# Feed-forward pairs: 18 of 22 by seven half-width products on operands scaled by 1/rms, the first four plain

## The chip, the cores and the metric

The kernel runs on one core of one Trainium2 chip. The metric is the device time of one execution in microseconds (us); the time shown for the kernel before is the median of three runs. The profile is one further execution, taken by the hardware profiler. In it PE is TensorE (matmuls), PEld its weight loads, DVE is VectorE, ACT ScalarE, POOL GpSimd, SP the queue that issues DMAs.

## The reference

Two layers over 512 tokens of width 1024. Each layer adds half a feed-forward, then a mixer (sparse attention, spatial gating, two gated projections), then half a second feed-forward; a last RMSNorm follows. What the change touches is the feed-forward:

```python
def rmsnorm(x, g):
    y = x * rsqrt(mean(x * x, axis=-1, keepdims=True) + 1e-6)
    return y * g

def swiglu(h, w_gate_up, w_down):              # 1024 -> 2 * 2816 -> 1024
    g, u = split(h @ w_gate_up, 2, axis=-1)
    return (silu(g) * u) @ w_down

x = x + 0.5 * swiglu(rmsnorm(x, ffn1_norm[l]), ffn1_w_gate_up[l], ffn1_w_down[l])
```

## The kernel before

**Layout.** x stays in SBUF transposed: eight tiles (`x[:, k, :]`) of 128 features by 512 tokens. The 2816 hidden features are 22 blocks of 128; a *pair* is the gate block and the up block of one such index, and its 1024x256 weights come in one buffer `X` of 128x2048.

**Three products for one.** All large matmuls run on fp32r operands. Each operand is split in a high part (a rounding copy on ACT) and the rest (a subtraction on DVE; `split`), and a product is high x high, high x low and low x high, all summed in PSUM by `chain`. So each weight tile costs one ACT and one DVE instruction before TensorE can use it.

**Pairs.** `pair_plain` makes gate and up as two chains of 8 x 3 matmuls of 512 columns, 48 in all. DVE multiplies both by `rbc` (1/rms broadcast over the partitions), ACT takes Silu, GpSimd multiplies the two. `pair_seven` treats the pair as a product of 2x2 blocks by Strassen's scheme in Winograd's form: seven products of half the depth and half the tokens, each 4 x 3 matmuls of 256 columns, 84 in all. For it DVE also adds weight blocks (`Sm`, tile names W here: one add of 1024 and two of 512 columns) and splits them (three of 1024 and one of 512 columns, the last one into VL); four DVE additions join the products from PSUM in `TT` (names YB). GpSimd then multiplies `TT` by `rbc` in two instructions, ACT takes Silu, GpSimd multiplies gate by up. The input side of the seven products (`norm_sums`: four sums of halves for each of four tile pairs, split into `Th`, `Tl`) is made once a feed-forward, after pair 0, from two ACT copies scaled by the gain.

**Order.** The operand tiles `xh`, `xl` hold the input times the gain, without 1/rms, so that matmuls start before the norm is known. 22 pairs come in the groups of `CHUNKS`, (0,6), (6,12), (12,18), (18,22). After each group its rows of the down projection run: 8 output tiles, each a chain of 3 matmuls of 512 columns for every pair of the group, added to x by DVE. `SEVEN` says which pairs run by seven products: of every three the first two, from pair 4 on in the first layer-half and 3 in the others, up to 20. That is 11 or 12 of 22 and 47 of 88 in all; 41 are plain. In the last group every new x tile is squared (ACT) and added to `ss0` (GpSimd for tiles 1 to 5, DVE for 6 and 7; `norm_square`), and the next operands are made.

**The planner.** All instructions are recorded, and `order` issues them by a list schedule over all engines: among those that its cost model (`SBUF_COST`, `cost`) takes for ready, the earliest in program order, weight preparation 100 places early. Each engine then runs its list in that fixed order. Buffers are rings: weights use two `X`, one `Sm`, three high and three low tiles of 1024 columns and one pair of 512; PSUM has six banks for the pairs and two for the down projection.

Of the kernel before, what the change touches and what calls it, by code (L numbers as in the profile page):

```python
# [20 lines left out]
NT = 4  # L21
DEPTH = 2
NG = (3 * DEPTH + 1) * KD
CHUNKS = ((0, 6), (6, 12), (12, 18), (18, 22))
LAG = 1
AHEAD = 100
FIRST, LATER = 4, 3

def SEVEN(j, begins):

    return j % 3 < 2 and (FIRST if begins else LATER) <= j < 21


NEG = -1e30
# [5 lines left out]

SBUF_COST = {"DVE": (154, 1.05), "ACT": (205, 0.835), "POOL": (150, 3.2)}
TABLES = {AF.Silu: 1, AF.Gelu_apprx_tanh: 2, AF.Exp: 3, AF.Tanh: 3, AF.Sqrt: 4}


# [96 lines left out]
class Recorder:  # L145
# [31 lines left out]
    def note(self, engine, op, args, kw):  # L177
        outs = [v for v in [args[0], kw.get("accum_out")] if isinstance(v, View)]
        ins = [v for v in list(args[1:]) + [v for k, v in kw.items() if k != "accum_out"] if isinstance(v, View)]
        i, deps = len(self.ops), set()  # L180
        for v, writes in [(v, False) for v in ins] + [(v, True) for v in outs]:
            assert v.live(), v.buf.name
            q, e = v.region()
            keep = []
            for j, jw, jq, je in v.buf.log:
                if (writes or jw) and jq & q and je & e:
                    if j != i:
                        deps.add(j)
                    if writes and jq & ~q == 0 and je & ~e == 0:
                        continue  # L190
                keep.append((j, jw, jq, je))
            keep.append((i, writes, q, e))
            v.buf.log = keep
        self.ops.append((engine, op, args, kw, deps, i + self.bias.get(engine, 0) - self.ahead, self.cost(engine, op, args, kw, outs, ins)))

    def cost(self, engine, op, args, kw, outs, ins):

# [25 lines left out]
    def order(self):  # L223
        ops = self.ops
        users, left = [[] for _ in ops], [len(o[4]) for o in ops]
        for i, o in enumerate(ops):
            for j in o[4]:
                users[j].append(i)
        ready = [0.0] * len(ops)
        free = dict.fromkeys(self.real, 0.0)  # L230
        cand = {e: [] for e in self.real}
        table, out, dma = 0, [], 0.0
        for i, o in enumerate(ops):
            if not left[i]:
                cand[o[0]].append(i)
        while len(out) < len(ops):
            best = None
            for e, c in cand.items():
                if not c:
                    continue  # L240
                t = max(free[e], min(ready[i] for i in c))
                if best is None or t < best[0]:
                    best = t, e
            t, e = best
            i = min((i for i in cand[e] if ready[i] <= t), key=lambda i: ops[i][5])
            cand[e].remove(i)
            busy, lat = ops[i][6]
            if e == "ACT":
                f = next((a for a in list(ops[i][2]) + list(ops[i][3].values()) if a in TABLES), None) \
                    if ops[i][1] == "activation" else None  # L250
                if f is not None and TABLES[f] != table:
                    table, busy, lat = TABLES[f], busy + 1283, lat + 1283
            if e == "SP":
                dma = max(dma, t + 2000) + lat
                lat = dma - t
            free[e] = t + busy
            out.append(i)
            for u in users[i]:
                same = ops[u][0] == e
                ready[u] = max(ready[u], t + (busy if same and e != "SP" else lat + 70))  # L260
                left[u] -= 1
                if not left[u]:
                    cand[ops[u][0]].append(u)
        self.span = max(free.values())
        return out
# [14 lines left out]
def trunk(ctx: ExitStack, tc, d):  # L280
# [20 lines left out]
    def units(*bufs):  # L301
        return [(b, c) for b in bufs for c in range(0, b.cols, 1024)]

    def halves(*bufs):
        return [(b, c) for b in bufs for c in range(0, b.cols, 512)]

    for tag, places, cols, dtype in (
            ("Xraw", [(W[0], 0), (W[1], 0)], 2048, F32), ("Fraw", units(W[0], W[1]), 1024, F32),
            ("S", [(W[2], 0)], 2048, F32), ("T32", [(W[3], 0)], 1024, F32), ("Txa", [(W[4], 0)], S, F32), ("Txb", [(W[4], 512)], S, F32), ("ss0", [(W[4], 1536)], S, F32),
            ("Fhi", units(*WH), 1024, F32R), ("Flo", units(*WL), 1024, F32R),  # L310
            ("F22h", halves(V[1])[:2], S, F32R), ("F22l", halves(V[1])[2:], S, F32R),
            ("raw", units(W[0], W[1])[:3], 1024, F32), ("whi", units(*WH), 1024, F32R), ("wlo", units(*WL)[:2], 1024, F32R),
            ("raw5", units(W[0], W[1])[:3] + units(W[3]), 1024, F32), ("wlo3", units(*WL), 1024, F32R),
            ("whi5", units(*WH, RB[0], RB[1]), 1024, F32R), ("wlo5", units(*WL, RB[2], RB[3]), 1024, F32R),
            ("U", [(W[2], 0)], 2048, F32), ("pA", halves(W[3]), S, F32), ("pB", halves(W[4]), S, F32),
            ("ga", halves(W[1])[2:] + [(G, 0)], S, F32), ("diagh", [(WL[2], 0)], S, F32R), ("diagl", [(WL[2], 512)], S, F32R)):
        rec.over(tag, places, cols, dtype)
    for k in range(24):
        rec.over(f"R{k}", [(RB[k // 2], k % 2 * 512)], S, F32R)
    for k, place in enumerate([(b, 0) for b in RB[6:]] + units(V[0])):  # L320
        rec.over(("Th", "Tl")[k // 4] + str(k % 4), [place], 1024, F32R)
    rec.over("TT", units(YB), 1024)
    rec.over("tm", [p for p, *_ in [rec.rings["t"]]][0] + halves(W[4]), S)
    for k in range(KD):
        rec.ring(f"xh{k}", 1, S, F32R)
# [17 lines left out]
    def tt(name):  # L343
        return rec.tile(st["t"], [P, S])
# [49 lines left out]
    def norm_begin(gidx):  # L394
        st["g"] = gains[:, gidx * KD:(gidx + 1) * KD]
        st["xh"], st["xl"] = [None] * KD, [None] * KD
        st["Th"], st["Tl"] = [None] * 4, [None] * 4
        st["s"] = None

    def norm_square(k):  # L400

        if st["s"] is None:
            st["s"] = rec.tile("ss0", [P, S])
            act(st["s"], x[:, k, :], AF.Square)
        else:
            sq = tt("sq")
            act(sq, x[:, k, :], AF.Square)
            eng = pool if k < 6 else vec
            eng.tensor_tensor(st["s"], st["s"], sq, op=ALU.add)

    def norm_operand(k):
# [5 lines left out]
        act(xh, x[:, k, :], AF.Copy, scale=g)  # L417
        vec.scalar_tensor_tensor(xl, x[:, k, :], g, f(xh), op0=ALU.mult, op1=ALU.subtract)

    def norm_sums(q):  # L420

        t, xa, xb = rec.tile("T32", [P, 1024]), rec.tile("Txa", [P, S]), rec.tile("Txb", [P, S])
        act(xa, x[:, q, :], AF.Copy, scale=st["g"][:, q:q + 1])
        act(xb, x[:, q + 4, :], AF.Copy, scale=st["g"][:, q + 4:q + 5])
        n1, n2, t3, t4 = (t[:, n * 256:(n + 1) * 256] for n in range(4))
        vec.tensor_tensor(n1, xa[:, 0:256], xa[:, 256:512], op=ALU.subtract)
        vec.scalar_tensor_tensor(n2, xb[:, 256:512], -1.0, n1, op0=ALU.mult, op1=ALU.subtract)
# [83 lines left out]
        nb[0] += 1  # L511
        return bank(nb[0] % 6, "ps_gu")

    def pair_plain(w):
        out = []
        for p, q in (("21", "22"), ("11", "12")):
            ps = next_bank()
# [5 lines left out]
            chain(ps, ops)  # L523
            out.append(ps)
        g, u = tt("g"), tt("u")
        vec.tensor_tensor(g, out[0], rbc, op=ALU.mult)
        act(g, g, AF.Silu)
        vec.tensor_tensor(u, out[1], rbc, op=ALU.mult)
        pool.tensor_tensor(u, u, g, op=ALU.mult)
        return u  # L530

    def pair_seven(w):
# [33 lines left out]
        vec.tensor_tensor(L[:, 256:512], D[:, 0:256], R[:, 256:512], op=ALU.add)  # L566
        times(A[:, 256:512], "s1", "n1")
        vec.tensor_tensor(half(R), half(R), two(A[:, 256:512]), op=ALU.add)
        for v, r in ((L, rbc[:, 0:256]), (R, rbc[:, 256:512])):
            pool.tensor_tensor(half(v), half(v), two(r), op=ALU.mult)  # L570
        u = tt("u")
        t4 = TT.rearrange("p (a b c) -> p a b c", a=2, b=2)
        act(t4[:, :, 1, :], t4[:, :, 1, :], AF.Silu, scale=-1.0)
        pool.tensor_tensor(half(u), t4[:, :, 0, :], t4[:, :, 1, :], op=ALU.mult)
        return u

    def ffn(gu, dn, l, gnext):
        st["rings"] = ("Fraw", "Fhi", "Flo")
        norm_finish(7)
        for c0, c1 in CHUNKS:  # L580
            hh, hl = [], []
            for j in range(c0, c1):
                seven = SEVEN(j, gnext == 1)
                w = first.pop() if first else pair_split(pair_load(gu[l, j]), seven)
                u = (pair_seven if seven else pair_plain)(w)
                if j == 0:
                    for q in range(4):
                        norm_sums(q)
                h = rt(2 * (j % 6), "hh")
                lo = rt(2 * (j % 6) + 1, "hl")  # L590
                split(h, lo, u)
                hh.append(h)
                hl.append(lo)
            last = c1 == 22
            final = last and gnext == 3 * DEPTH
            nk, fin = c1 - c0, []
# [2 lines left out]
            for dd in range(KD):  # L599
# [21 lines left out]
                        norm_rows(fin[-1], lo // P, 2, sq)  # L621
                if last and not final:
                    norm_prep(dd)
            for half, ps in enumerate(fin):
                store(half, ps)

# [598 lines left out]
```

## Time and profile before

| | |
|---|---|
| three runs, median (range) | 2168.75 us (2167.99 to 2169.68) |
| profiled execution: time, span | 2171.32 us, 2169.4 us |
| granted TensorE clock, mean | 0.996 |
| PE, PEld, DVE, ACT, POOL busy | 99%, 85%, 70%, 47%, 17% |

The span reaches from the first to the last instruction; the execution's time is 1.9 us longer. Matmuls are pipelined and the end of each is modelled, so two matmuls in a row overlap in the trace: what one costs in a stream is the time from its start to the start of the next. The same holds in a smaller measure for DVE. All instructions carry line 276, since the planner issues them there; tiles tell them apart.

### The profile page before, as it was taken

The page shows a single profiled execution, that of the slowest core. Times are in us where ns is not written, and L with a number is a line of the kernel's source. Part 1 is how long each engine was busy: PE and PEld are TensorE (multiplying, and loading weights), DVE is VectorE, ACT ScalarE, POOL GpSimd, SP SyncE. Part 2 cuts the span into 40 slices and gives each one's busy share as a digit, 9 for nine tenths or more (in the row PEclk, how much of TensorE's full clock was granted, in tenths as well). Part 3 has the DMA queues.
Part 4 walks back from the last instruction along what each step waited for, and adds up shares of the span by engine and source line. Part 5 has one row for each costly group of instructions (what it writes and reads, how often), then busy time and mean ns, then how long its engine had stood idle before and what let it go on. Part 6 is the DMA issues. An engine that isn't in the chain of part 4 may idle for free.

```text
span 2169.4 us, 30061 instructions
## 1 busy us (share of the span) xinstructions
PE 2139.0 (99%) x11704; PEld 1849.9 (85%) x11704; DVE 1518.8 (70%) x2357; ACT 1011.9 (47%) x1635; POOL 379.6 (17%) x261
## 2 busy tenths in 40 slices
PE   8999999999999999999999999999999999999998
PEld 6898987888878889898888988878888788898986
DVE  7685767678885757585685775685888758585764
ACT  6343334676653533343453433357766436343434
POOL 2131322010000122231311413210100001231411
PEclk9999999999999999999999999999999999999999
DMA  5323333421113323323333232234111233323232
GB/s 191 115 88 107 91 100 114 149 62 47 59 59 124 104 89 106 109 88 107 89 100 113 88 115 87 91 109 160 49 58 50 69 107 97 112 86 114 85 101 68
DMA packets 65664, 209.25 MB, mean 96 GB/s; under 512 B 7793, under 2 KB 8305, under 8 KB 65521
## 3 DMA queue, kind: packets, MB, share of 16 engines
q1 hardware_dynamic: 65520, 207.32, 30.7%
q8 instruction: 92, 1.51, 0.3%
q14 instruction: 52, 0.42, 0.1%
HBM read 205.19 MB, written 2.10 MB: 96 GB/s over the span
## 4 chain that ended last, share of the span: by engine, by line
PE 93%; DVE 4%; ACT 2%; issue 1%; DMA 0%; SPq 0%; DVEq 0%; ACTq 0%
PE b L276 93%; DVE W L276 1%; DVE RB L276 1%; DVE WL L276 1%; DVE xl L276 1%; DVE x L276 1%; ACT WH L276 0%; ACT xh L276 0%; DMA x<-in_x_dram 0%; ACT t L276 0%; ACT L276 0%; ACT RB L276 0%; DVE t L276 0%; DVE YB L276 0%; DVE sm L276 0%
## 5 line engine op out<-in xcount | busy, mean ns | idle before, releaser
L276 ACT ACTIVATE WH<-W 128x1024 fp32r<-128x1024 f32 (+4 forms) x458 | 446.5, 976 | 636.5 <-PE b L276 553.4
L276 DVE TENSOR_TENSOR WL<-W,WH 128x1024 fp32r<-128x1024 f32 (+4 forms) x458 | 528.8, 1157 | 185.1 <-ACT WH L276 122.4
L276 PE MATMUL b<-xh,WH 128*128 128x512 f32 (+1 forms) x1716 | 608.5, 359 | 10.2 <-ACT xh L276 9.3
L276 PE MATMUL b<-xl,WH 128*128 128x512 f32 (+1 forms) x1716 | 608.5, 358 | 0.0
L276 PE MATMUL b<-RB,WH 128*128 128x512 f32 (+2 forms) x2270 | 579.7, 349 | 0.4
L276 PE MATMUL b<-xh,WL 128*128 128x512 f32 (+1 forms) x1716 | 568.8, 358 | 1.4 <-DVE WL L276 1.4
L276 PEld LDWEIGHTS b<-RB,WH 128*128 128x128 f32 x2270 | 397.9, 189 | 57.0 <-DVE x L276 2.1
L276 PE MATMUL b<-RB,WL 128*128 128x512 f32 (+1 forms) x1276 | 391.5, 341 | 0.0
L276 PEld LDWEIGHTS b<-xh,WH 128*128 128x128 f32 x1716 | 326.3, 190 | 56.6 <-ACT xh L276 9.7
L276 PEld LDWEIGHTS b<-xl,WH 128*128 128x128 f32 x1716 | 326.1, 190 | 45.5 <-DVE xl L276 1.1
L276 PEld LDWEIGHTS b<-xh,WL 128*128 128x128 f32 x1716 | 315.8, 190 | 46.6 <-DVE WL L276 2.3
L276 POOL TENSOR_TENSOR YB<-YB,rbc 128x512 f32<-128x512 f32 x94 | 168.6, 1812 | 671.3 <-DVE YB L276 671.3
L276 PEld LDWEIGHTS b<-RB,WL 128*128 128x128 f32 x1276 | 231.7, 190 | 27.3
L276 DVE SCALAR_TENSOR_TENSOR x<-b,x 128x512 f32<-128x512 f32 (+1 forms) x145 | 99.5, 686 | 166.6 <-PE b L276 166.6
L276 PE MATMUL b<-VH,WH 128*128 128x256 f32 (+1 forms) x426 | 136.3, 321 | 4.9 <-DVE W L276 4.9
L276 ACT ACTIVATE RB<-t 128x512 fp32r<-128x512 f32 (+3 forms) x120 | 67.7, 574 | 124.4 <-POOL t L276 112.5
L276 DVE TENSOR_TENSOR t<-b,rbc 128x512 f32<-128x512 f32 (+1 forms) x90 | 61.3, 687 | 91.6 <-PE b L276 91.3
L276 PE MATMUL b<-RB,RB 128*128 128x512 f32 (+4 forms) x478 | 124.8, 346 | 0.0
L276 POOL TENSOR_TENSOR t<-t,t 128x512 f32<-128x512 f32 x41 | 65.6, 1601 | 315.5 <-DVE t L276 253.0
L276 POOL TENSOR_TENSOR W<-W,t 128x512 f32<-128x512 f32 x35 | 49.3, 1409 | 403.0 <-ACT t L276 402.7
L276 DVE TENSOR_TENSOR RB<-t,RB 128x512 fp32r<-128x512 f32 (+3 forms) x120 | 77.0, 649 | 48.2 <-ACT RB L276 47.8
L276 DVE TENSOR_TENSOR W<-W 128x1024 f32<-128x1024 f32 (+3 forms) x87 | 97.7, 1122 | 5.6 <-ACT W L276 2.7
(161 smaller groups left out, 2443.7 us busy)
## 6 DMA issues: line engine op xcount, KB each, us to landing
W<-in_gu_dram SPq DMA_DIRECT2D x176, 512.0 KB, 3.7
W<-in_dn_dram SPq DMA_DIRECT2D x96, 384.0 KB, 3.1
W<-in_wA_dram SPq DMA_DIRECT2D x48, 512.0 KB, 3.5
W<-in_phi_dram SPq DMA_DIRECT2D x16, 512.0 KB, 4.5
W<-in_dn_dram SPq DMA_DIRECT2D x32, 256.0 KB, 2.7
W<-in_wo_dram SPq DMA_DIRECT2D x16, 512.0 KB, 3.5
W<-in_wv_dram SPq DMA_DIRECT2D x8, 512.0 KB, 4.2
W<-in_wu_dram SPq DMA_DIRECT2D x8, 512.0 KB, 5.3
```

Of the source, the lines that this page charges most:

```text
L276: getattr(self.real[engine], op)(*args, **kw)
```

## The change

A first group of four plain pairs, on unscaled operands as before, then three groups of six pairs, all by seven products, in all four feed-forwards: 72 pairs by seven products and 16 plain. After pair 1, `norm_scaled` makes eight tiles `xn` = x times gain times `rbc` (one DVE instruction each). `norm_sums` takes its halves from them, so its ACT copies go. While the first group's down projection runs, `norm_again` splits `xn` into the same buffers `xh`, `xl`. From then on no pair is multiplied by `rbc`. The product of gate and up moves from GpSimd to DVE for every pair, and so do the additions of squares. The planner gets another cost for GpSimd and treats its instructions and DVE's with two SBUF inputs as users of one port.

```diff
-CHUNKS = ((0, 6), (6, 12), (12, 18), (18, 22))
+CHUNKS = ((0, 4), (4, 10), (10, 16), (16, 22))
-FIRST, LATER = 4, 3
-def SEVEN(j, begins):
-    return j % 3 < 2 and (FIRST if begins else LATER) <= j < 21
+SCALED = CHUNKS[0][1]
+def SEVEN(j):
+    return 4<=j<22
-SBUF_COST = {"DVE": (154, 1.05), "ACT": (205, 0.835), "POOL": (150, 3.2)}
+SBUF_COST = {"DVE": (154, 1.05), "ACT": (205, 0.835), "POOL": (190, 2.15)}
...
+                         engine == "POOL" or engine == "DVE" and sum(not v.buf.psum and v.ids.size >= 256 for v in ins) > 1))
...
+            if ops[i][7]:
+                start = max(t, port)
+                port = start + busy
+                busy, lat = busy + start - t, lat + start - t
...
-            eng = pool if k < 6 else vec
+            eng = vec
...
+    def norm_scaled(k):
+        st["xn"][k] = rec.tile(f"xn{k}", [P, S])
+        vec.scalar_tensor_tensor(st["xn"][k], x[:, k, :], st["g"][:, k:k + 1], rbc, op0=ALU.mult, op1=ALU.mult)
+    def norm_again(k):
+        st["xh"][k], st["xl"][k] = rec.tile(f"xh{k}", [P, S]), rec.tile(f"xl{k}", [P, S])
+        split(st["xh"][k], st["xl"][k], st["xn"][k])
     def norm_sums(q):
-        t, xa, xb = rec.tile("T32", [P, 1024]), rec.tile("Txa", [P, S]), rec.tile("Txb", [P, S])
-        act(xa, x[:, q, :], AF.Copy, scale=st["g"][:, q:q + 1])
-        act(xb, x[:, q + 4, :], AF.Copy, scale=st["g"][:, q + 4:q + 5])
+        t, xa, xb = rec.tile("T32", [P, 1024]), st["xn"][q], st["xn"][q + 4]
...
+        if scaled:
+            act(g, out[0], AF.Silu)
+            vec.tensor_tensor(u, out[1], g, op=ALU.mult)
+            return u
...
-        pool.tensor_tensor(u, u, g, op=ALU.mult)
+        vec.tensor_tensor(u, u, g, op=ALU.mult)
...
-        for v, r in ((L, rbc[:, 0:256]), (R, rbc[:, 256:512])):
-            pool.tensor_tensor(half(v), half(v), two(r), op=ALU.mult)
...
-        pool.tensor_tensor(half(u), t4[:, :, 0, :], t4[:, :, 1, :], op=ALU.mult)
+        vec.tensor_tensor(half(u), t4[:, :, 0, :], t4[:, :, 1, :], op=ALU.mult)
...
-                if j == 0:
-                    for q in range(4):
-                        norm_sums(q)
...
+                if j == 1:
+                    for k in (0, 4, 1, 5, 2, 6, 3, 7):
+                        norm_scaled(k)
+                if 2 <= j < SCALED and j < 5:
+                    norm_sums(j - 2)
...
+                if c0 == 0:
+                    norm_again(dd)
+                    if dd % 2 == 0 and st["Th"][dd // 2] is None:
+                        norm_sums(dd // 2)
```

## Rows read from the trace of the kernel before

**Rows 1.** The page's first lines: the span, the busy time of each engine with its share of the span, the granted TensorE clock in 40 slices of the span (tenths of full speed), and the chain of work that ended last, by engine.

```profile
span 2169.4 us, 30061 instructions
...
PE 2139.0 (99%) x11704; PEld 1849.9 (85%) x11704; DVE 1518.8 (70%) x2357; ACT 1011.9 (47%) x1635; POOL 379.6 (17%) x261
...
PEclk9999999999999999999999999999999999999999
...
PE 93%; DVE 4%; ACT 2%; issue 1%; DMA 0%; SPq 0%; DVEq 0%; ACTq 0%
```

**Rows 2.** What TensorE waited for over the whole span: total us, times, the longest one.

```profile
PE b L276 <- ACT xh L276: 9.3, 2, 8.1
PE b L276 <- DVE W L276: 7.2, 4, 2.7
PE b L276 <- DVE WL L276: 1.4, 2, 0.7
```

**Rows 3.** Two stages of the span: the second feed-forward of the first layer, and the mixer of the second layer. Columns: stretch, its length, then busy us (instructions) of each engine, the granted clock as a share, the DMA share, GB/s.

```profile
742.00:1082.00 340.00, 339.90 (x1972) 301.41 (x1971) 227.39 (x271) 131.35 (x172) 85.33 (x51) 1.00 0.32 99
...
1437.00:1814.00 377.00, 370.81 (x1849) 307.57 (x1848) 286.66 (x605) 226.31 (x449) 18.32 (x15) 1.00 0.27 86
```

**Rows 4.** The first feed-forward, the same columns: a down projection of six pairs, then two pairs by seven products, then one plain pair.

```profile
77.07:109.71 32.64, 32.64 (x145) 27.04 (x144) 17.02 (x22) 8.51 (x11) 1.29 (x1) 1.00 0.38 121
109.71:129.87 20.16, 20.16 (x170) 20.15 (x169) 18.53 (x21) 8.67 (x11) 5.42 (x3) 1.00 0.32 98
129.87:140.77 10.90, 10.90 (x50) 9.01 (x49) 7.53 (x9) 4.51 (x7) 4.80 (x3) 1.00 0.34 109
```

**Rows 5.** Timeline of TensorE in the first feed-forward: the first matmul of pair 4, the first pair by seven products; of pair 6, the first of two by seven products; of pair 8, plain; and of pair 9. Columns: start, duration, what it is.

```profile
56.09 0.28 PE L276 MATMUL b<-xh,WH 128*128 128x256 f32 x1
...
109.71 0.28 PE L276 MATMUL b<-xh,WH 128*128 128x256 f32 x1
...
129.87 0.40 PE L276 MATMUL b<-xh,WH 128*128 128x512 f32 x1
...
140.77 0.28 PE L276 MATMUL b<-xh,WH 128*128 128x256 f32 x1
```

**Rows 6.** Timeline of VectorE in the first two seven-product pairs and the start of the plain pair (start, duration, out<-in; in brackets the idle time before it and what ended it).

```profile
111.81 1.23 DVE L276 TENSOR_TENSOR W<-W 128x1024 f32<-128x1024 f32 x1
113.07 0.69 DVE L276 TENSOR_TENSOR W<-W,W 128x512 f32<-128x512 f32 x1
113.68 1.22 DVE L276 TENSOR_TENSOR WL<-W,WH 128x1024 fp32r<-128x1024 f32 x1
114.82 0.69 DVE L276 TENSOR_TENSOR W<-W,W 128x512 f32<-128x512 f32 x1
115.42 0.68 DVE L276 TENSOR_TENSOR YB<-b,t 128x512 f32<-128x512 f32 x1
...
119.15 0.42 DVE L276 TENSOR_TENSOR YB<-b,YB 128x256 f32<-128x256 f32 x1
119.48 0.68 DVE L276 TENSOR_TENSOR VL<-W,VL 128x512 fp32r<-128x512 f32 x1
120.08 0.68 DVE L276 TENSOR_TENSOR YB<-YB,b 128x512 f32<-128x512 f32 x1
...
122.46 2.21 DVE L276 TENSOR_TENSOR W<-W 128x1024 f32<-128x1024 f32 x1
...
126.29 1.21 DVE L276 TENSOR_TENSOR WL<-W,WH 128x1024 fp32r<-128x1024 f32 x1
127.42 0.68 DVE L276 TENSOR_TENSOR YB<-b,t 128x512 f32<-128x512 f32 x1
128.03 0.68 DVE L276 TENSOR_TENSOR W<-W,W 128x512 f32<-128x512 f32 x1
128.62 0.68 DVE L276 TENSOR_TENSOR RB<-t,RB 128x512 fp32r<-128x512 f32 x1
129.23 0.68 DVE L276 TENSOR_TENSOR YB<-b,YB 128x512 f32<-128x512 f32 x1
```

**Rows 7.** Groups of instructions by shape, whole span: engine, operation, out<-in, shapes, xcount | busy us, mean ns of one | idle time before them and what ended most of it.

```profile
L276 POOL TENSOR_TENSOR YB<-YB,rbc 128x512 f32<-128x512 f32 x94 | 168.6, 1812 | 671.3 <-DVE YB L276 671.3
...
L276 DVE TENSOR_TENSOR WL<-W,WH 128x768 fp32r<-128x768 f32 x96 | 91.4, 953 | 47.0 <-ACT WH L276 47.0
...
L276 POOL TENSOR_TENSOR t<-YB 128x512 f32<-128x512 f32 x47 | 69.6, 1482 | 36.1 <-ACT YB L276 36.1
...
L276 ACT ACTIVATE RB<-t 128x512 fp32r<-128x512 f32 x88 | 55.2, 628 | 112.5 <-POOL t L276 112.5
...
L276 POOL TENSOR_TENSOR W<-W,t 128x512 f32<-128x512 f32 x35 | 49.3, 1409 | 403.0 <-ACT t L276 402.7
...
L276 ACT ACTIVATE YB<-YB 128x512 f32<-128x512 f32 x47 | 29.5, 627 | 68.0 <-POOL YB L276 68.0
...
L276 DVE TENSOR_TENSOR xl<-W,xh 128x512 fp32r<-128x512 f32 x16 | 10.3, 686 | 2.9 <-ACT xh L276 2.9
L276 ACT ACTIVATE xh<-W 128x512 fp32r<-128x512 f32 x16 | 10.1, 633 | 8.7 <-DVE W L276 7.3 <-PE b L276 1.0
```

**Rows 8.** Two groups by tile: the operand split that scales by the gain, and the copy that makes the broadcast 1/rms; duration in ns as min/median/max, first and last start in us.

```profile
L276 DVE SCALAR_TENSOR_TENSOR xl<-x,gains,xh x48: 737/747/1790, 8.1 to 1808.7; 128x512 fp32r<-128x512 f32 x48
...
L276 DVE COPY rbc<-b x6: 691/692/692, 32.7 to 1814.9; 128x512 f32<-128x512 f32 x6
```

More of the change, by code (lines that the diff above doesn't have):

```diff
@@ L193, in note @@
             v.buf.log = keep
-        self.ops.append((engine, op, args, kw, deps, i + self.bias.get(engine, 0) - self.ahead, self.cost(engine, op, args, kw, outs, ins)))
+        self.ops.append((engine, op, args, kw, deps, i + self.bias.get(engine, 0) - self.ahead, self.cost(engine, op, args, kw, outs, ins),
+                         engine == "POOL" or engine == "DVE" and sum(not v.buf.psum and v.ids.size >= 256 for v in ins) > 1))
     def cost(self, engine, op, args, kw, outs, ins):
@@ L231, in order @@
         cand = {e: [] for e in self.real}
-        table, out, dma = 0, [], 0.0
+        table, out, dma, port = 0, [], 0.0, 0.0
         for i, o in enumerate(ops):
@@ L308, in trunk @@
             ("Xraw", [(W[0], 0), (W[1], 0)], 2048, F32), ("Fraw", units(W[0], W[1]), 1024, F32),
-            ("S", [(W[2], 0)], 2048, F32), ("T32", [(W[3], 0)], 1024, F32), ("Txa", [(W[4], 0)], S, F32), ("Txb", [(W[4], 512)], S, F32), ("ss0", [(W[4], 1536)], S, F32),
+            ("S", [(W[2], 0)], 2048, F32), ("T32", [(W[3], 0)], 1024, F32), ("ss0", [(W[4], 1536)], S, F32),
             ("Fhi", units(*WH), 1024, F32R), ("Flo", units(*WL), 1024, F32R),
@@ L322, in trunk @@
     rec.over("TT", units(YB), 1024)
+    for k, place in enumerate(halves(W[3])[2:] + halves(W[4])[:3] + [(G, 0)] + rec.rings["tb"][0]):
+        rec.over(f"xn{k}", [place], S)
     rec.over("tm", [p for p, *_ in [rec.rings["t"]]][0] + halves(W[4]), S)
@@ L396, in norm_begin @@
         st["xh"], st["xl"] = [None] * KD, [None] * KD
-        st["Th"], st["Tl"] = [None] * 4, [None] * 4
+        st["Th"], st["Tl"], st["xn"] = [None] * 4, [None] * 4, [None] * KD
         st["s"] = None
@@ L512, in next_bank, with pair_plain @@
         return bank(nb[0] % 6, "ps_gu")
-    def pair_plain(w):
+    def pair_plain(w, scaled):
         out = []
@@ L582, in ffn @@
             for j in range(c0, c1):
-                seven = SEVEN(j, gnext == 1)
+                seven = SEVEN(j)
                 w = first.pop() if first else pair_split(pair_load(gu[l, j]), seven)
-                u = (pair_seven if seven else pair_plain)(w)
-                if j == 0:
-                    for q in range(4):
-                        norm_sums(q)
+                u = pair_seven(w) if seven else pair_plain(w, j >= SCALED)
                 h = rt(2 * (j % 6), "hh")
```

## The prediction

> **What bounds the kernel now.** I read the page's first lines, then TensorE's waits, then stages and single pairs. TensorE is busy for 2139.0 of 2169.4 us at the full granted clock, and 93% of the chain that ended last is TensorE [rows 1]. Busy alone proves little, since the ends of matmuls are modelled; the waits do. TensorE's longest are 9.3 us, of which 8.1 stand before its first matmul, and 7.2 us in four waits on DVE [rows 2]. A feed-forward stage has it busy for 339.90 of 340 us [rows 3]. So what TensorE streams in a feed-forward is what it costs. The other engines only have to keep up: DVE is busy for 18.53 of the 20.16 us of two neighbouring pairs by seven products, but for only 17.02 of 32.64 us in a down projection [rows 4]. Both matter for a change that puts six such pairs in a row.
>
> **TensorE's term.** Two pairs by seven products take 129.87 - 109.71 = 20.16 us, 10.08 each, and a plain pair 140.77 - 129.87 = 10.90 us [rows 5]. That is 0.120 us for each of 84 matmuls and 0.227 us for each of 48. A pair that changes over saves 0.82 us. There are 88 - 16 = 72 such pairs after, 47 before, so 25 change over: -20.5 us. The down projections keep their 88 x 24 matmuls.
>
> The Trainium skill (TensorE: Matmul & The Clock Gate, section Back-to-back issue gap) has a matmul at full clock start every N/2.4 + 2.5 ns, 216 ns at 512 columns and 109 at 256. By that page the term would be an estimated 30 us (48 x 0.216 against 84 x 0.109, times 25); the rows are 11 ns longer at either width, and the sum goes by them.
>
> **DVE in a run of six.** Cost in a stream is from start to start [rows 6]: 1.14 us for a split of 1024 (113.68 to 114.82), 1.26 for the wide add of weights (111.81 to 113.07), 0.61 for an operation of 512 (128.03 to 128.62), 0.33 for 256 (119.15 to 119.48). Weights of one pair: three splits 3.42, the wide add 1.26, two adds 1.21, the small split 0.60, together 6.49. Behind the products: three joins of 512 and one of 256, 2.13; new on DVE the gate times up, 0.61, in place of GpSimd's 1.48 [rows 7]; the split of the result, 0.61; together 3.35. So 9.84 us a pair against TensorE's 10.08. By the printed durations (1.22, 1.23, 0.69, 0.42 [rows 6]) it would be 10.78.
>
> GpSimd's three instructions a pair go (two of 1.81 and one of 1.48 us [rows 7]). Where one runs beside DVE, DVE stretches: the same wide add takes 2.21 us in the second pair and 1.23 in the first [rows 6]. That loss goes too, but none of it is on TensorE's path now: the pair in which it falls still takes 10.08. I count nothing for it.
>
> A run of six pairs lasts 60.5 us. In it DVE prepares five pairs (the first one's weights, all but the last split, come during the down projection before, where DVE has 15.6 us free): 5 x 6.49 + 1.1; it finishes six, 20.1; and it splits two tiles of down weights at 0.95 [rows 7]: 55.6 us, so 4.9 are free. By durations the same sum is 60.9, or 0.4 over. A wait of TensorE inside a run is therefore bounded by nothing and by about 0.7 us a pair (10.78 less 10.08). I take nothing: two such pairs in a row now run without any wait although GpSimd stretches DVE there.
>
> **The end of a run.** The last pair of a run now needs, after its last product: a join 0.68, Silu 0.63, gate times up 0.68, ACT's copy 0.63, the subtraction 0.68, so 3.3 us before the sixth pair's rows of the down projection can start. TensorE has five pairs of the first output tile to work on, 15 x 0.227 = 3.4 us, and the second bank's tile behind it. If the second tile's weights come late, hand-offs show: I take 0.2 us for each of 12 runs, +2.4; with no cover it would be 3.3 each.
>
> **The first group.** New on DVE and ACT: `norm_scaled`, eight instructions, nearest 0.75 us [rows 8]; `norm_again`, eight ACT copies of 0.63 and eight subtractions of 0.69 [rows 7]. Eight scaled ACT copies go from `norm_sums`. The rewriting of `xh` must wait for pair 3's reads, and pair 4 for the rewriting: 8 x 0.63 + 0.69 = 5.8 us, while the down projection of four pairs gives 96 x 0.227 = 21.8. Hidden; uncovered it would be 23 us in four feed-forwards. In the first feed-forward it is tight: `rbc` exists only from 32.7 us [rows 8], and pair 4, at 56.09 before [rows 5], comes 21.8 later, at 77.9. In these 45 us DVE has four pairs' ends 9.8, two pairs' splits 4.6, `norm_scaled` 6.0, `norm_sums` 4 x (4 x 0.33 + 1.14) = 9.8, eight down tiles of a split and an addition 9.8, `norm_again` 4.9 and pair 4's weights 5.4: 50 us. Five are too many, ten by durations; the first two products need no sums (2.9 us) and other orders help. I take +3 once, between 0 and 10. The later feed-forwards have `rbc` at their start, and the 65.4 us of their first group (4 x 10.90 + 21.8) hold this work: 0.
>
> **The rest.** 35 additions of squares go from GpSimd's 1.41 to DVE's 0.61. An output tile of the last group takes TensorE 18 x 0.227 = 4.1 us, DVE there 0.95 + 0.69 + 0.61 + 0.75 = 3.0. The last two additions were on DVE already: 0, uncovered 0.6 at each of seven norms. In the mixers the planner's new costs only reorder; GpSimd is busy 18 us there, and TensorE idle 377.00 - 370.81 = 6.2 us in one [rows 3]. That idle time could vanish or double, so between -12 and +12 over both; I take 0, since 18 us of 377 touch little.
>
> **Sum.** -20.5 + 2.4 + 3 = -15.1. The profiled execution took 2171.3 us (span 2169.4), so 2156.2 in its like; the runs' median is 2.6 us lower, 2168.75, so 2153.6, rounded to 2153.5.
>
> **Rivals.**
> Likeliest, 0.70: as summed, own range 2146 to 2159.
>
> DVE falls a little behind inside the runs, 0.5 us a run more: 6 us, 2159.6; at 0.9 us a run 2164. For it: 9.84 against 10.08 leaves no room for a DVE that stands still while it waits for ACT or for a freed buffer. Against: 4.9 us free over the run. 0.10.
>
> Slower: DVE becomes the bound in the runs. If it works at its printed durations and nothing is prepared ahead, a pair takes 10.78: 72 x 0.70 = 50 us lost, 20.5 won, 2198. It decides from 20.5 / 72 = 0.28 us lost a pair. For it: the second pair's DVE rows in the trace stand almost without a gap. Against: there it was stretched by GpSimd and TensorE did not wait. 0.09. The Trainium skill (Perfetto Trace Analysis, section Optimizing Scalar/DVE Operations) speaks for this rival, since it would move work off a saturated DVE, even to GpSimd, and this change moves it on; the same section adds that the two share a read port so that moving may not help, and the stretched rows agree.
>
> No change: the rewriting of operands is mostly not hidden, say 12 to 20 of its 23 us: 2166 to 2174. For it: it stands between two groups whose order is fixed. Against: 21.8 us of cover. 0.05.
>
> The planner's new order costs the mixers up to 12 us: 2165. 0.06, half of it faster by enough.
>
> 0.2% is 4.3 us, about what a measurement tells from no change. Faster by more: 0.70 + 0.10 + 0.03 = 0.83; the same 0.05 + 0.03 = 0.08; slower 0.09. The range takes in the slight lag of DVE and most of the mixers' case, and downward 8 us for a first feed-forward without its 3, run ends without their 2.4 and a few us won in the mixers: 2145 to 2165.
>
> **What would show it.** Right: 72 x 84 + 16 x 48 matmuls in pairs; six pairs of 60.5 us; GpSimd idle in the feed-forwards, and no wide add above 1.3 us; a TensorE wait near 78 us of about 3. Wrong: TensorE waits on WL, VL or W in the second half of the runs (DVE binds); waits on `xh` between the first and second group (rewriting); waits on RB at the start of down projections above 0.2 us; a mixer longer than 377.

## The result, and the profile after

The changed kernel takes 2135.45 us in the median of four runs (2135.19 to 2137.64) against 2168.9 for the kernel before in the same session: a ratio of 0.9848, interval 0.9831 to 0.9865. It is faster, by 33.4 us and not by the 15.1 forecast, and ends 9.6 us below the low end of the range. The profiled execution took 2135.27 us, 36.0 less than the profiled one before.

The page's first lines of the kernel after, as [rows 1] before, with the chain that ended last:

```profile
span 2133.5 us, 32011 instructions
...
PE 2111.9 (99%) x12610; PEld 1874.1 (88%) x12610; DVE 1696.4 (80%) x2719; ACT 1064.6 (50%) x1710; POOL 28.0 (1%) x44
...
PE 97%; DVE 2%; DMA 0%; ACT 0%; issue 0%; SPq 0%; DVEq 0%; ACTq 0%
```

TensorE has 906 more instructions; 25 pairs at 84 - 48 = 36 more matmuls make 900 of them. DVE's share goes from 70 to 80%, GpSimd's from 17 to 1%. The chain is now 97% TensorE where it was 93%. What TensorE waited for in the kernel after (total us, times, longest), the answer to [rows 2]:

```profile
PE b L281 <- ACT xh L281: 7.7, 1, 7.7
PE b L281 <- DVE WL L281: 2.9, 3, 1.2
PE b L281 <- DVE W L281: 0.8, 1, 0.8
PE b L281 <- DVE pc L281: 0.7, 1, 0.7
```

The four waits on DVE W, 7.2 us, have become one of 0.8. (Tile names are shared: at the end of a feed-forward W is the sum of squares, in a mixer a tile of the spatial gating; WH and WL are a weight's high part and its rest, and in a feed-forward RB holds the split results that the down projection reads.) Waits like these, and the matmuls behind them, are where the forecast went wrong. Here are four stretches of the kernel after, with the columns of [rows 3]: a run of six pairs by seven products, the down projection behind it, then the second feed-forward and the second mixer whole.

```profile
172.18:232.66 60.48, 60.48 (x506) 60.47 (x505) 55.10 (x71) 28.82 (x38) 0.00 (x0) 1.00 0.27 86
232.66:265.32 32.66, 32.66 (x146) 27.03 (x145) 18.38 (x24) 9.99 (x13) 0.00 (x0) 1.00 0.41 133
729.22:1072.81 343.59, 343.48 (x2229) 314.95 (x2227) 281.55 (x379) 155.14 (x205) 0.00 (x0) 1.00 0.32 102
1421.02:1782.83 361.81, 359.34 (x1807) 299.76 (x1806) 276.32 (x584) 214.90 (x433) 12.67 (x10) 1.00 0.26 83
```

And the last two stages of the kernel before, cut at the same matmuls:

```profile
741.47:1093.48 352.01, 350.80 (x2015) 309.89 (x2014) 236.97 (x288) 140.06 (x184) 85.33 (x51) 1.00 0.33 99
1447.70:1813.79 366.09, 361.10 (x1805) 299.93 (x1803) 276.19 (x588) 218.36 (x439) 18.32 (x15) 1.00 0.26 83
```

The run of six takes 60.48 us (60.5 forecast) with DVE busy for 55.10 (55.6 forecast) and no idle TensorE. The feed-forward won 8.4 us. The mixer won 4.3, and of its arithmetic nothing was edited but the engine of five additions of squares (GpSimd 15 instructions before, 10 after).

Idle rows understate a wait, since the modelled end of a matmul covers part of it. So I took what each matmul costs beyond its pace in a stream (0.227 us at 512 columns, 0.120 at 256, 0.174 at 384, 0.130 at 280, start to start). The sum of that excess, in us by stage, is worked out from all TensorE rows. An "end" is from the last group's down projection to the next stage; the kernels to the right of "after" are those of experiments 2, 3 and 4:

```
                              before  after  planner  after with  squares  groups
                                             alone    old planner alone    alone
four feed-forwards' groups       4.9    7.5     5.3      7.4        5.3    17.0
four ends                       11.6    2.8     4.6      2.8        5.4     2.5
two mixers                      25.8   16.4    18.3     23.5       27.8    25.9
all                             42.5   26.6    28.2     33.6       38.6    45.3
```

Before to after: stream -20.5 (the pairs that changed over), groups +2.6, ends -8.8, mixers -9.4. That is -36.1, and the span is 35.9 shorter. The forecast had the first term right, +5.4 for the second and zero for the other two.

### The profile page after: what moved, and what is told of

Same layout as the page of the kernel before. It is cut to its first block, busy times and chain, and to the rows that moved or that the text cites. A ratio compares the mean times of both kernels' runs of the same rounds, so it can differ in the third digit from the quotient of the medians.

```text
span 2133.5 us, 32011 instructions
## 1 busy us (share of the span) xinstructions
PE 2111.9 (99%) x12610; PEld 1874.1 (88%) x12610; DVE 1696.4 (80%) x2719; ACT 1064.6 (50%) x1710; POOL 28.0 (1%) x44
## 4 chain that ended last, share of the span: by engine, by line
PE 97%; DVE 2%; DMA 0%; ACT 0%; issue 0%; SPq 0%; DVEq 0%; ACTq 0%
PE b L281 97%; DVE W L281 1%; DVE t L281 0%; DVE WL L281 0%; DVE RB L281 0%; DMA W<-in_gu_dram 0%; DMA x<-in_x_dram 0%; DVE x L281 0%; DVE YB L281 0%; ACT RB L281 0%; ACT WH L281 0%; DVE rbc L281 0%; DVE VL L281 0%; ACT VL L281 0%; SPq L281 0%
## 5 line engine op out<-in xcount | busy, mean ns | idle before, releaser
L281 ACT ACTIVATE WH<-W 128x1024 fp32r<-128x1024 f32 (+2 forms) x483 | 471.3, 981 | 632.2 <-PE b L281 490.9
L281 PE MATMUL b<-RB,WH 128*128 128x512 f32 (+1 forms) x2724 | 667.2, 338 | 0.4
L281 DVE TENSOR_TENSOR WL<-W,WH 128x1024 fp32r<-128x1024 f32 (+2 forms) x483 | 541.4, 1128 | 115.7 <-PE b L281 55.9
L281 PE MATMUL b<-xh,WH 128*128 128x256 f32 (+1 forms) x1616 | 531.9, 335 | 8.0 <-ACT xh L281 7.7
L281 PE MATMUL b<-xl,WH 128*128 128x256 f32 (+1 forms) x1616 | 531.4, 335 | 0.0
L281 PEld LDWEIGHTS b<-RB,WH 128*128 128x128 f32 x2724 | 467.8, 190 | 55.6 <-DVE x L281 2.4
L281 PE MATMUL b<-xh,WL 128*128 128x256 f32 (+1 forms) x1616 | 494.0, 337 | 2.3 <-DVE WL L281 2.3
L281 PE MATMUL b<-RB,WL 128*128 128x256 f32 (+1 forms) x1578 | 463.1, 330 | 0.6 <-DVE WL L281 0.6
L281 PE MATMUL b<-RB,VL 128*128 128x256 f32 x720 | 117.6, 283 | 0.2 <-ACT RB L281 0.2
L281 PEld LDWEIGHTS b<-VH,WH 128*128 128x128 f32 x576 | 109.9, 191 | 7.8 <-DVE W L281 2.0
L281 DVE TENSOR_TENSOR W<-W,W 128x512 f32<-128x512 f32 (+1 forms) x159 | 108.5, 682 | 3.1
```

Source lines behind the costliest of these rows:

```text
L281: getattr(self.real[engine], op)(*args, **kw)
```

## Experiments

The kernel after was timed in the first session only. In the later ones the median of the kernel before was 2170.1 to 2171.4 us, not 2168.9, so a difference from the kernel after is known to about 2.5 us; ratios are to the kernel before in the same session.

**1. The stream.** One pair of each run of six plain again, 12 in all:

```diff
-    return 4<=j<22
+    return 4 <= j < 22 and j % 6 != 3
```

> The kernel after with three pairs of each feed-forward (9, 15 and 21, the last of each run) plain again, 12 in all. If the feed-forwards cost what TensorE streams: 12 x 0.82 = 9.8 us slower, 2145.3. If DVE held the runs back, the relief of DVE would give part of that back: 2138 to 2142.

2145.67 us, 10.2 above the kernel after: 0.85 a pair, where [rows 5] gave 0.82. The traces agree: the second feed-forward of this kernel takes 346.00 us, that of the kernel after 343.59, so 0.80 for each of three pairs. The stream term stands, and DVE did not hold the runs back.

**2. The planner's two edits alone, in the kernel before** (the new cost of GpSimd and the shared port; arithmetic untouched):

```diff
-"POOL": (150, 3.2)
+"POOL": (190, 2.15)
...
+            if ops[i][7]:
+                start = max(t, port)
+                port = start + busy
```

> The kernel before with only the planner's two edits (the GpSimd cost and the shared port). Theory P (the planner's new model orders the mixers better, where the waits of TensorE fell from 25.4 to 15.6 us with the whole change): about 10 us faster, 2159, the gain inside the two mixers, the feed-forwards unchanged. Rival L (the mixers' waits fell because of what GpSimd no longer does): within 2 us of 2168.9.

2157.94 us against 2170.12, ratio 0.9942 (0.9928 to 0.9957): -12.2 us from the order of instructions alone. By stage -7.5 in the mixers and -7.0 at the ends, so the forecast gain is right but half of it lies where this expectation had not put it.

**3. The kernel after with the old planner** (the same lines undone):

> The kernel after with the planner's two edits undone. Theory P: about 10 us slower than the kernel after, 2145, the waits back in the mixers. Rival L: within 2 us of 2135.5.

2142.33 us, 0.987 (0.9855 to 0.9885) of before: the planner is worth 6.9 us here, all in the mixers (23.5 against 16.4 of excess); the ends stay as they are. So without the planner's edits the change is worth -27.8 us, with nothing else -12.2; together -33.4, since both take away most of the ends' waits.

**4. Squares to DVE alone, and new groups alone, in the kernel before:**

```diff
-            eng = pool if k < 6 else vec
+            eng = vec
```

> The kernel before with only the additions of squares moved from GpSimd to DVE. Theory L (GpSimd's slow additions, and DVE's stretched ones beside them, made TensorE wait at the ends of the feed-forwards, 8.8 us in three ends before and 1.2 after): 5 to 8 us faster, 2161 to 2164, gained at those ends. Rival W (the wider last group, 4.1 instead of 2.7 us a down tile, gives those ends time): within 2 us of 2168.9.

2166.15 us, 0.9979 (0.997 to 0.9989).

```diff
-CHUNKS = ((0, 6), (6, 12), (12, 18), (18, 22))
+CHUNKS = ((0, 4), (4, 10), (10, 16), (16, 22))
```

> The kernel before with only the groups of the kernel after, (0,4), (4,10), (10,16), (16,22); the same pairs by seven products as before. Rival W: 5 to 8 us faster, 2161 to 2164, the waits at the ends of the feed-forwards gone. Theory L: within 2 us of 2168.9.

2173.84 us, 1.0014 (1.0005 to 1.0023). Neither expectation holds alone: either edit takes most of the waits at the ends away (11.6 to 5.4 and to 2.5 us). The groups alone add 12.1 us in the feed-forwards, more than they win. Neither helps the mixers (27.8 and 25.9 against 25.8). So three edits, these two and the planner's, each remove most of the same waits.

The first feed-forward's end shows why. VectorE of the kernel before, one GpSimd row, start and duration, and the TensorE row that waits (`x<-b,x` adds an output tile to x, `W<-W,t` adds a square, `xl` is the next operand):

```profile
357.40 2.44 DVE L276 SCALAR_TENSOR_TENSOR xl<-x,gains,xh 128x512 fp32r<-128x512 f32 x2
...
361.31 1.42 POOL L276 TENSOR_TENSOR W<-W,t 128x512 f32<-128x512 f32 x1 [2.69 <-ACT t L276]
...
361.82 1.47 DVE L276 SCALAR_TENSOR_TENSOR xl<-x,gains,xh 128x512 fp32r<-128x512 f32 x1 [0.24 <-ACT xh L276]
363.20 0.68 DVE L276 SCALAR_TENSOR_TENSOR x<-b,x 128x512 f32<-128x512 f32 x1
363.81 1.21 DVE L276 TENSOR_TENSOR WL<-W,WH 128x1024 fp32r<-128x1024 f32 x1
364.94 0.68 DVE L276 TENSOR_TENSOR W<-W,t 128x512 f32<-128x512 f32 x1
365.54 0.74 DVE L276 SCALAR_TENSOR_TENSOR xl<-x,gains,xh 128x512 fp32r<-128x512 f32 x1
366.20 0.68 DVE L276 SCALAR_TENSOR_TENSOR x<-b,x 128x512 f32<-128x512 f32 x1
366.81 1.21 DVE L276 TENSOR_TENSOR WL<-W,WH 128x1024 fp32r<-128x1024 f32 x1
367.94 0.68 DVE L276 TENSOR_TENSOR W<-W,t 128x512 f32<-128x512 f32 x1
...
368.67 1.05 PE L276 MATMUL b<-ones,W 128*128 128x1 f32 x8 [1.25 <-DVE W L276]
```

One round of DVE (addition to x, a weight split of the next stage, square, operand) takes 3.00 us, 364.94 to 367.94. An output tile of a last group of four pairs gives 12 x 0.227 = 2.72. So DVE falls behind at the last two tiles. At the five before them the square is GpSimd's, and there its addition stretches DVE (1.47 for the operand at 361.82, while GpSimd adds from 361.31; 2.44 for two of them at 357.40, where one alone takes 0.74). The sum of squares comes late and TensorE waits. The stretching seems the larger part: with all squares on DVE, which adds 0.61 us of its own at each of those five tiles, only 5.4 of the 11.6 us were left. The same place in the kernel after:

```profile
350.50 0.69 DVE L281 SCALAR_TENSOR_TENSOR x<-b,x 128x512 f32<-128x512 f32 x1 [1.11 <-PE b L281]
351.19 1.23 DVE L281 TENSOR_TENSOR WL<-W,WH 128x1024 fp32r<-128x1024 f32 x1
352.33 0.69 DVE L281 TENSOR_TENSOR W<-W,t 128x512 f32<-128x512 f32 x1
352.93 0.74 DVE L281 SCALAR_TENSOR_TENSOR xl<-x,gains,xh 128x512 fp32r<-128x512 f32 x1
354.58 0.69 DVE L281 SCALAR_TENSOR_TENSOR x<-b,x 128x512 f32<-128x512 f32 x1 [0.90 <-PE b L281]
```

Now a tile gives 18 x 0.227 = 4.08 us (350.50 to 354.58) and DVE waits 0.90 in it. A group of six pairs at the end makes that room; the planner's edits alone, with four pairs there and GpSimd's squares, took away as much (7.0 us) by order.

**5. Which of the planner's edits.** The new cost alone, then the port alone, in the kernel before:

> The kernel before with only the planner's cost of a GpSimd instruction changed (1.29 us at 512 columns instead of 1.79). Theory C (the cost is what matters, since the planner took GpSimd for slower than it is): 8 to 12 us faster, 2157 to 2161. Theory Q (the shared port is what matters, since the costly waits in the mixers stood behind a DVE instruction held up by GpSimd): within 3 us of 2169.

2170.65 us, 0.9996 (0.9987 to 1.0006): no change.

> The kernel before with only the planner's shared port. Theory Q: 8 to 12 us faster, 2157 to 2161. Theory C: within 3 us of 2169.

2181.28 us, 1.0045 (1.0028 to 1.0061): slower. Both theories fail; only both edits together gain. With the port and two other costs, higher and lower:

```diff
-"POOL": (150, 3.2)
+"POOL": (210, 2.3)
```

> The kernel before with the planner's shared port and a GpSimd cost 0.1 us above the measured one (1.39 us at 512 columns, where the change has 1.29 and before had 1.79). If the port helps wherever the cost is near the measured one: 2156 to 2161 like the two edits together. If the gain of the two edits is one lucky order: anywhere between 2157 and 2181, and the mixers' waits anywhere between 18 and 28 us.

```diff
-"POOL": (150, 3.2)
+"POOL": (170, 2.0)
```

> The kernel before with the planner's shared port and a GpSimd cost 0.1 us below the measured one (1.19 us at 512 columns). If the port helps wherever the cost is near the measured one: 2156 to 2163, the mixers' waits 18 to 21 us. If it is the luck of one order: up to 2181, the waits up to 28.

2162.02 us, 0.996 (0.9944 to 0.9976), and 2157.7 us, 0.9936 (0.9916 to 0.9956). The mixers' excess is 20.1 and 18.1 us, beside 18.3 in experiment 2; without the port it was 23.5 to 27.8 in six kernels, with the port and the old cost 27.9. The higher cost ends 1 us above the range of the port theory, and the ranges of the other theory take in both times, so luck is not excluded; but the gain doesn't hang on the exact figure, which makes one lucky order unlikely. The old cost gives GpSimd 150 + 512 x 3.2 = 1788 ns for 512 columns; its additions of squares took 1409 [rows 7], and the new cost gives 1291. My reading is that a port reserved for too long postpones the wrong things; that is argued.

What one such place looks like, in the first mixer before (GpSimd and VectorE, and the TensorE row that waits):

```profile
458.51 1.58 POOL L276 TENSOR_TENSOR t<-t,G 128x512 f32<-128x512 f32 x1 [4.62 <-ACT t L276]
...
459.12 2.23 DVE L276 TENSOR_TENSOR RB<-W,RB 64x512 fp32r<-64x512 f32 x2 [0.18 <-ACT RB L276]
...
462.53 0.39 PE L276 MATMUL b<-VH,WH 128*128 128x256 f32 x1 [2.19 <-DVE W L276]
```

and the windows around it (busy us by engine, then the granted clock):

```profile
460.00:462.30 2.30, 0.34 (x2) 0.00 (x0) 2.24 (x4) 1.45 (x3) 0.09 (x1) 1.00 0.72 224
462.30:464.50 2.20, 1.97 (x13) 1.93 (x14) 2.14 (x6) 1.66 (x3) 0.00 (x0) 0.87 0.00 0
464.50:467.20 2.70, 2.70 (x9) 2.12 (x8) 2.67 (x5) 2.08 (x3) 0.43 (x1) 0.50 0.00 0
```

After, GpSimd's product starts earlier against DVE's work and the pair of splits is not stretched:

```profile
450.48 1.70 POOL L281 TENSOR_TENSOR t<-t,G 128x512 f32<-128x512 f32 x1 [3.23 <-ACT t L281]
...
453.29 1.41 DVE L281 TENSOR_TENSOR RB<-W,RB 64x512 fp32r<-64x512 f32 x2
```

```profile
452.00:467.20 15.20, 15.20 (x98) 13.53 (x97) 14.91 (x23) 11.00 (x18) 3.61 (x4) 1.00 0.20 70
```

2.23 us against 1.41, a wait of 2.19 against none. The stretch is only 0.82 of that wait: in the kernel after TensorE also has matmuls on `xh` and `xl` to run until 455.8 us, when its first product on `VH` can start (455.88). So the order of TensorE's own work matters as much. With the old planner in the kernel after (experiment 3) the pair takes 2.23 again and the wait is back:

```profile
456.53 0.39 PE L276 MATMUL b<-VH,WH 128*128 128x256 f32 x1 [2.18 <-DVE W L276]
```

In the kernel before, the wait costs more than its length: behind it TensorE's clock is granted at 0.50, its lower level of 1.2 GHz, for some nine to twelve matmuls. Those of 512 columns start 0.43 us apart there (464.55, then 464.98), not 0.227, so a stretch costs about 1.6 us by my estimate. The kernel before has three of them (near 464, 1089 and 1537 us), each behind one of the four waits on DVE W; after has none but at its start and its end, which before has too. The wait of 2.18 us above, in experiment 3's kernel, had none behind it.

**6. A planner closer to the trace.** DVE and ACT rows start some 0.09 us before the row ahead ends [rows 6]. Told so, in the kernel after:

```diff
-        return t, t
+        return t - (87 if engine == "DVE" else 90 if engine == "ACT" else 0), t
```

> The kernel after with one more correction of the planner: a DVE or ACT instruction keeps its engine busy for 0.09 us less than it takes to finish, as the starts in the trace show. If orders made with truer costs have fewer waits: 3 to 8 us faster than after, 2127 to 2132, out of the 16 us of waits left in the mixers. If orders differ by luck: 2130 to 2145.

2156.94 us, 21.5 slower than the kernel after. The mixers' excess is 36.1 us. Waits and windows of the first mixer there:

```profile
PE b L281 <- DVE W L281: 2.2, 1, 2.2
```

```profile
452.50:455.00 2.50, 0.28 (x3) 0.05 (x1) 2.40 (x5) 1.22 (x3) 1.17 (x1) 1.00 0.36 105
455.00:459.00 4.00, 4.00 (x18) 3.71 (x19) 2.96 (x7) 1.72 (x3) 0.52 (x1) 0.58 0.17 68
```

The long wait and the low clock (0.58) are back. Neither expectation held, and truer costs of DVE and ACT gave more waits, not fewer. So what the other two edits won is not safe against a further edit of the model: each has to be tried.

**7. What taking GpSimd out is worth.** The kernel before with the new groups and 18 pairs by seven products, operands unscaled, GpSimd's three instructions a pair kept:

```diff
-    return j % 3 < 2 and (FIRST if begins else LATER) <= j < 21
+    return 4 <= j < 22
```

> The kernel before with only the pairs and groups of the kernel after: 18 pairs by seven products in runs of six, but operands unscaled and GpSimd's three instructions a pair in place. If TensorE's stream is all that counts: 2148. If GpSimd had to go before runs of six could hold: it stretches DVE by 2.5 to 3.4 us a pair in the trace of before, so DVE needs 11.7 to 12.6 us a pair against 10.08, and the end of a run is 4 us longer: 1.6 to 2.5 us lost in each of 72 pairs, 2263 to 2330 and more.

2240.28 us, 1.0316 (1.0295 to 1.0337): slower by 69, though not by the 94 and more that were expected. Its waits, the wide add and the wide splits (mean ns behind the comma), and one run with its down projection:

```profile
PE b L276 <- DVE WL L276: 61.4, 46, 2.7
```

```profile
L276 DVE TENSOR_TENSOR W<-W 128x1024 f32<-128x1024 f32 x72 | 130.2, 1808 | 3.2 <-DMA W<-in_gu_dram 1.1
L276 DVE TENSOR_TENSOR WL<-W,WH 128x1024 fp32r<-128x1024 f32 x346 | 480.3, 1390 | 88.3 <-PE b L276 30.2 <-issue 29.0 <-ACT WH L276 27.1
```

```profile
180.53:281.06 100.53, 96.06 (x650) 89.03 (x649) 81.07 (x88) 38.80 (x51) 29.54 (x18) 0.98 0.30 95
```

The same add and splits in the kernel after, with the product of gate and up that came to DVE:

```profile
L281 DVE TENSOR_TENSOR W<-W 128x1024 f32<-128x1024 f32 x72 | 87.8, 1220 | 0.4
L281 DVE TENSOR_TENSOR WL<-W,WH 128x1024 fp32r<-128x1024 f32 x346 | 420.7, 1224 | 101.0 <-PE b L281 45.5 <-ACT WH L281 40.4 <-issue 13.7
L281 DVE TENSOR_TENSOR t<-YB 128x512 f32<-128x512 f32 x72 | 49.4, 686 | 7.8 <-ACT YB L281 7.8
```

1.81 us on average against 1.22 for the add, 1.39 against 1.22 for a split, and 100.5 us for a run with its down projection against 60.48 + 32.66 = 93.1 (its mean clock of 0.98 is in that). The kernel of experiment 3, with the same pairs, groups and planner, but with scaled operands and no GpSimd in pairs and squares, is 98 us faster. The Trainium skill (SBUF — State Buffer, section Who interferes with whom) says that a DVE instruction with two SBUF inputs contends with a GpSimd instruction that reads SBUF, and these means agree. One of the three instructions put back, the seven-product pairs' gate times up:

```diff
-        vec.tensor_tensor(half(u), t4[:, :, 0, :], t4[:, :, 1, :], op=ALU.mult)
+        pool.tensor_tensor(half(u), t4[:, :, 0, :], t4[:, :, 1, :], op=ALU.mult)
```

> The kernel after with the gate times up of the pairs by seven products back on GpSimd. DVE has 0.61 us less a pair, GpSimd 1.3 to 1.5 more. If GpSimd hurts DVE more than the work it takes over: 5 to 20 us slower, 2140 to 2155, DVE instructions of two SBUF inputs above 1.3 us again. If it helps a DVE that has 2.4 us free a run: 2130 to 2135.

2149.93 us, 14.5 slower than the kernel after, as the first reading expected. The wide add, and a run:

```profile
L281 DVE TENSOR_TENSOR W<-W 128x1024 f32<-128x1024 f32 x72 | 125.1, 1738 | 1.1 <-DMA W<-in_gu_dram 0.3
```

```profile
888.55:949.02 60.47, 60.47 (x505) 60.47 (x504) 55.55 (x64) 29.38 (x39) 7.66 (x5) 1.00 0.26 86
```

Taken from GpSimd, a product costs DVE 0.69 us; left there, it stretches one add by 0.52 and itself takes 1.53. DVE is not relieved: it is busy for 55.55 us of the run with 64 instructions, beside 55.10 with 71. The time goes at the down projections (33.07 against 32.66 us behind this run) and in each feed-forward's first run. TensorE's new waits there are on RB (3.6 us in five), so the product's own 1.53 us on the way to RB is a second cause, which this run does not part from the stretching.

**8. How much room DVE has.** One more DVE addition of 512 in every seven-product pair of the kernel after, into a tile that nobody reads:

```diff
         vec.tensor_tensor(half(R), half(R), two(A[:, 256:512]), op=ALU.add)
+        vec.tensor_tensor(rec.tile("junk", [P, S]), L, R, op=ALU.add)
```

> The kernel after with one more DVE addition of 512 columns in each of the 72 pairs by seven products, into a tile that nobody reads: 0.61 us a pair, 3.7 a run. If the run as a whole must hold DVE's work (4.9 us free by the prediction's sum): within 2 us of 2135.5. If each pair must (0.24 us free of 10.08): (0.61 - 0.24) x 72 = 27 us slower, 2162.

2154.63 us, 19.2 slower. A run and its down projection:

```profile
887.09:947.56 60.47, 60.47 (x506) 60.47 (x504) 56.42 (x73) 28.55 (x38) 0.00 (x0) 1.00 0.25 81
947.56:981.12 33.56, 33.47 (x147) 26.80 (x145) 20.96 (x28) 9.69 (x14) 0.00 (x0) 1.00 0.41 139
```

The run holds its 60.47 us; the down projection is 0.9 longer. Over all twelve runs with their projections it is 0.9 to 2.4 each, 18.4 in all. Two readings remained: the last pair's addition lies on the path to the projection's rows, or the run's work spills over its end. So two and three additions in the first five pairs of each run alone:

> The kernel after with two more DVE additions of 512 columns, into a tile that nobody reads, in the first five pairs of each run of six and none in the last: 6.1 us a run. If the run as a whole must hold DVE's work, with 4.9 us free by the prediction's sum (5.4 us by the trace of after): 0.7 to 1.2 us a run, 8 to 14 us slower, 2144 to 2150. If each pair must: (1.22 - 0.24) x 60 = 59 us slower, 2194. If what the run before paid for was only the longer end of the last pair: within 2 us of 2135.5.

> The same with three additions in the first five pairs: 9.2 us a run. Run as a whole: 3.8 to 4.3 us a run, 45 to 52 us slower, 2181 to 2187. Each pair: (1.83 - 0.24) x 60 = 95 us slower, 2231. Only the end of the last pair: within 2 us of 2135.5.

2190.74 us (ratio 1.0093, 1.0078 to 1.0108) and 2235.18 (1.0297, 1.0282 to 1.0312). The waits with two:

```profile
PE b L281 <- ACT RB L281: 18.9, 13, 1.6
```

and one middle run with its down projection, with two and with three:

```profile
901.32:998.14 96.82, 95.04 (x650) 87.38 (x648) 80.20 (x104) 38.25 (x51) 0.00 (x0) 1.00 0.30 98
915.97:1017.19 101.22, 96.61 (x649) 88.55 (x648) 83.65 (x109) 38.49 (x51) 0.00 (x0) 0.98 0.30 94
```

They take 96.8 and 101.2 us in place of 93.1. So of 10 x 0.61 = 6.1 us added, 2.4 are absorbed, and of 9.2, 1.1; the work spills over even without the last pair's additions. Both times lie within 5 us of the expectation that each pair must hold its own work (2194 and 2231) and far from the other two; with one addition that expectation was 7 us too high. So the 4.9 us free that I worked out for a run were at most half there. The engine's own sum is right (55.10); that DVE's remaining time goes into waits for products and for ACT, and is no room, is my reading and not shown.

**9. One pair more by seven products** (groups of 3, 6, 6, 6 and 1):

```diff
-CHUNKS = ((0, 4), (4, 10), (10, 16), (16, 22))
+CHUNKS = ((0, 3), (3, 9), (9, 15), (15, 21), (21, 22))
-    return 4<=j<22
+    return 3 <= j < 22
```

> The kernel after with three plain pairs first and 19 by seven products, in groups (0,3), (3,9), (9,15), (15,21), (21,22). Four more pairs change over, so the stream is 3.3 us shorter. If it goes through: 2132. If the first group's down projection (16.3 us instead of 21.8) no longer covers the rewriting of the operands, or the last group of one pair leaves DVE eight more additions in too little time: 2140 or more.

2217.26 us, 82 slower than the kernel after, with these waits first:

```profile
PE b L281 <- ACT RB L281: 21.8, 9, 6.1
```

The runs in the middle still take 93.1 us. By the excess, some 50 us more than in the kernel after stand from the last group of one pair on, which gives 3 x 0.227 = 0.68 us a tile to 3.0 us of DVE: experiment 4's lack of room in the large. Another 25 stand ahead of the first runs, the other half of the expectation.

## Why the prediction was wrong

- **TensorE's term, -20.5:** right (experiment 1).
- **DVE in a run of six:** right in result (60.48 us without a wait, 55.10 of 55.6 busy); the 4.9 us free were mis-sized, 1.1 to 2.4 by experiment 8. The rival that DVE binds was nearer than its 0.09 suggests, and experiment 8 shows what it looks like.
- **GpSimd's stretching, "I count nothing":** true of the pairs before, but it was the condition of the whole forecast. With GpSimd kept, the same 18 pairs cost 69 us (experiment 7); without it, under the same planner, they won 28 (experiment 3).
- **Run ends, +2.4:** too much; the second to fourth feed-forward's groups have 0.3 to 0.4 us more of excess each. **First group, +3:** 1.6. The wait forecast near 78 us did not come. The rewriting is hidden: no TensorE wait on `xh` beyond the kernel's first.
- **"The rest", 0: the step that failed**, in both halves, for 18.2 us. For the squares I held DVE's 3.0 us a tile against after's 18 x 0.227 = 4.1 and found cover. I did not make the same sum for before, 12 x 0.227 = 2.7, though [rows 2] show the waits. There DVE had 3.0 at the last two tiles and rows stretched by GpSimd's squares at the others: too little cover, 11.6 us stood at the ends, and the change removed 8.8 of them (experiment 4). For the mixers I bounded the planner at 12 us either way and took 0, and the mixers won 9.4. The planner's edits are worth 7.1 to 7.5 of that (experiments 2 and 3); where the other 2 come from is open. Its bound held, but the range took in only a few us of it: with all 12 the low end would have been near 2141, and with the ends' 8.8 as well it would have held the time.
- **The lower clock behind a wait** was in neither sum. [Rows 2] put the four waits on DVE W at 7.2 us; they cost more, about 5 us by my estimate of 1.6 for each of three stretches at half speed.

What stays open: which rule of the planner decides in the mixers. The port with a cost near the trace's helps in four kernels (16.4 to 20.1 us of excess), each edit alone does not, and a truer cost of DVE and ACT undoes it. I have no account that covers all of these.

## What to carry to other kernels

Make every cover sum for the kernel before as well as for the one after: a wait that stands in the rows of before can be removed by an edit that was made for something else, and a list of waits says which to ask about. Where an automatic planner's costs change, put its bound into the range on both sides and don't call it zero; the order alone moved this kernel by 12 us one way and, from the other end, 21 the other. An instruction taken off GpSimd was worth more here than its own time, because it stopped stretching DVE's; that showed only once DVE had little room left, in runs of six.

## What the runs showed of the hardware

Three of the four waits on DVE W (2.2, 1.1 and 2.7 us) in an otherwise dense TensorE stream were followed by matmuls at half speed; the one of 1.25 us was not, and neither was one of 2.18 us in the kernel of experiment 3. At the end of the second feed-forward before, TensorE waited 1.11 us, ran eight matmuls of one column, and its clock fell:

```profile
1088.70:1093.50 4.80, 4.80 (x16) 3.79 (x15) 2.49 (x6) 4.77 (x7) 0.00 (x0) 0.66 0.17 67
```

The mean of 0.66 lies between the levels of 1.2 and 2.4 GHz; single matmuls there last 0.63 us, beside 0.40 at full clock. In the kernel after the eight one-column matmuls of that end come without a wait (1068.68 us) and the clock stays at 1.00.
